# Other start places in SBUF, by 4 to 64 bytes, for the matmul operands of the SwiGLU stages of a float32r decoder trunk

## The chip, the cores and the metric

The kernel runs on one core of one Trainium2 chip. The metric is the device time of one execution in microseconds. A profiled execution is slightly shorter in its span (first to last instruction) than in the time that is reported for it.

## The reference

The reference is a decoder trunk of two layers on 256 positions of 1024 channels, all in float32. A layer is a first SwiGLU block, a mixer, and a second SwiGLU block:

```python
x = x + 0.5 * swiglu(rms_norm(x, ffn1_norm[l]), ffn1_w_gate[l], ffn1_w_up[l], ffn1_w_down[l])
...
x = x + merged @ w_out[l]
x = x + 0.5 * swiglu(rms_norm(x, ffn2_norm[l]), ffn2_w_gate[l], ffn2_w_up[l], ffn2_w_down[l])

def swiglu(x, w_gate, w_up, w_down):
    return (jax.nn.silu(x @ w_gate) * (x @ w_up)) @ w_down
```

Gate and up have 1024 x 2816 weights, down has 2816 x 1024. The mixer (a forgetting attention and a gated recurrence beside each other) is not touched by the change.

## The kernel before

**Products.** Every large product is made of three matmuls in float32r. Each operand is split into a high part, rounded to float32r, and a low part, the rest: `mm3` (L256) issues high weights with high activations, high weights with low activations, and low weights with high activations, all into one PSUM bank. A matmul has 128 x 128 weights and 256 columns of activations, which are all 256 positions; each issues its own weight load, as the profile's PEld counts show.

**Weights.** SyncE brings 1 MB pieces of weights from HBM into the three buffers `wr`. `split_half` (L378) splits one half piece, 128 x 1024, at a time: ScalarE casts it to the high part and VectorE subtracts to get the low part (`split`, L280). The parts lie in tiles of 1088 elements a partition: eight tiles `W`, or tiles of the pool of 21 called `R` when no two W tiles are idle. A part takes up 1024 of the 1088 elements, and `where` (L374) says from which element: the pair in `self.spots`, or `AT = 16, 48`, that is 64 B for the high part and 192 B for the low part. The bases of all W and R tiles are multiples of 128 B in the built program. The q, k and v projections of the mixer have (0, 0); there the weights are the moving operand, with 512 columns.

**A SwiGLU stage** (`ffn`, L607). There are four: `ffn1` and `ffn2` in both layers. The 22 blocks of 128 hidden channels each have a gate half and an up half, of 8 x 3 matmuls each, which makes 1056 matmuls for gate and up. The moving operand is `xs`, the normalised input in both parts. `glu` (L657) takes the two banks: VectorE scales the gate's, ScalarE applies SiLU, VectorE multiplies with up, and `split` writes h in two parts into an `R` tile that holds two blocks: high of the first block at element 0, low at 256, high of the second at 512, low at 768. Then the down product runs over 8 blocks of output channels, each over the 22 blocks of h: 528 matmuls, whose moving operand is h. `FFN_AT` (L59) is the pair of places for all weights of these stages, the same as `AT`.

**What sets the order.** The program is written out by a planner that runs a model of the engines' clocks (`Clock`, L66) and emits work when operands are due (`run`, L401). Its model has names and sizes of tiles, not addresses.

**The start.** `setup` (L515) issues `WARM` = 9 float32 matmuls of zeros on TensorE while the first weights are on their way. The profile records each as two.

Of the kernel before, what the change touches and what calls it, by code (L numbers as in the profile page):

```python
# [24 lines left out]
F32R = mybir.dt.float32r  # L25
# [5 lines left out]
NF = F // 128  # L31
# [2 lines left out]
OFF = {"q": 0, "k": 1024, "v": 2048, "f": 3072, "xr": 3080, "gr": 4104, "gA": 5128, "gR": 6152}  # L34
PROJ = [("q", 0), ("k", 0), ("v", 0), ("q", 1), ("k", 1), ("v", 1)]

MIX = [('q',0),('k',0),('xr',0),('v',0),('xr',1),('q',1),('k',1),('v',1),('gr',0),('gr',1),('gA',0),('gA',1),('gR',0),('gR',1)]

P_G = {"ffn1": 0, "mix": 8, "ffn2": 16}
P_QN, P_KN, P_CW, P_CB, P_BA, P_BX, P_BGA, P_BGM, P_LAM, P_BXR, P_BGR, P_BV, NP_ = 24, 25, 26, 58, 66, 74, 82, 90, 98, 106, 114, 122, 130  # L40
LEAD = 5
WARM = 9
EARLY = -0.6
ROOM = 3.5
FLEX = 4
# [7 lines left out]
EARLYX = -0.4  # L53
CALM = 2, 3
NEAR = 8
SIDES = False

AT = 16, 48
FFN_AT = AT  # L59


def f32(ap):
# [138 lines left out]
class Trunk:  # L201
# [199 lines left out]
    def run(self):  # L401
# [8 lines left out]
        for s, st in enumerate(steps):  # L410
# [6 lines left out]
            ends = any(lab == "x" for st in steps[max(0, s - CALM[1]):s + CALM[0]] for _, lab in st.done)  # L417
            while (j < n and first[j] - s <= (NEAR if ends else AHEAD) and self.split_places()
                   and self.clock.done[self.raw[j // 2].tensor.name] <= self.now + EARLY
# [95 lines left out]
    def setup(self):  # L515
# [16 lines left out]
        warm = self.take(self.banks)  # L532
        for _ in range(WARM):
            self.PE.matmul(warm[:, 0:128], self.cpad, self.cpad, start=True, stop=True)
# [72 lines left out]
    def ffn(self, l, name):  # L607
        st = {}
        phase = self.phase
        self.phase += 1  # L610

        def gu_steps(f):
            js = self.half(), self.half()
            self.spots.update(dict.fromkeys(js, FFN_AT))
            banks = {}

            def step(i, ks):
                def fn(wh, wl):
                    if ks[0] == 0:

                        self.need(lambda: phase in self.rb or len(self.banks.idle) > 1, "stats", "x")
                        banks[i] = self.take(self.banks)
                    for k in ks:
                        w = slice(k * 128, k * 128 + 128)
                        self.product(banks[i], wh[:, w], wl[:, w], self.x_rhs(phase, k), k == 0, k == 7, SIDES)
                return Step(js[i], fn, [(self.glu(f, phase, banks, st), "glu")] if i and ks[-1] == 7 else [])
            if f == 0 and not self.steps:
                order = [(i, ks) for ks in (range(4), range(4, 8)) for i in range(2)]
            elif f == 0:
                order = [(0, range(4)), (0, range(4, 7)), (1, range(4)), (1, range(4, 7)), (0, range(7, 8)), (1, range(7, 8))]  # L630
            else:
                order = [(i, ks) for i in range(2) for ks in (range(4), range(4, 8))]
            self.steps += [step(i, ks) for i, ks in order]

        for f in range(NF):
            gu_steps(f)
        halves = [self.half() for _ in range(NF)]
        self.spots.update(dict.fromkeys(halves, FFN_AT))
        runs = {}
        for i in range(8 * NF):  # L640
            d, f = divmod(i, NF)
            runs.setdefault((halves[i // 8], d, i // 4), []).append((i % 8, f))

        def down(half, d, blocks):
            def fn(wh, wl):
                for i, f in blocks:
                    if f == 0:
                        st["acc", d] = self.take(self.banks)
                    self.need(lambda: ("h", f) in st, "glu", "stats", "x")
                    w = slice(i * 128, i * 128 + 128)  # L650
                    self.product(st["acc", d], wh[:, w], wl[:, w], st["hT", f // 2][:, f % 2], f == 0, f == NF - 1, SIDES)
                    if d == 7 and f % 2:
                        self.big.give(st.pop(("tile", f // 2)))
            return Step(half, fn, [(self.ffn_end(l, name, phase, d, st), "x")] if blocks[-1][1] == NF - 1 else [])
        self.steps += [down(half, d, blocks) for (half, d, _), blocks in runs.items()]

    def glu(self, f, phase, banks, st):  # L657
        if phase not in self.rb:
            yield self.when(must=lambda: phase in self.rb)
            yield self.when(self.rb[phase])  # L660
        s2 = self.take(self.small)
        g, h = s2[:, 0:256], s2[:, 256:512]
        self.DVE.tensor_mul(g, self.total(banks[0], SIDES), self.rb[phase])
        self.banks.give(banks[0])
        self.ACT.activation(g, g, AF.Silu)
        yield self.when(s2)

        self.DVE.tensor_mul(h, self.total(banks[1], SIDES), g)
        self.banks.give(banks[1])
        if ("hT", f // 2) not in st:  # L670
            st["tile", f // 2], st["hT", f // 2] = self.slot([2, 512], F32R)
        hT = st["hT", f // 2][:, f % 2]
        yield self.when(s2)
        self.split(hT[:, 0:256], hT[:, 256:512], h)
        self.small.give(s2)
        st["h", f] = True

    def ffn_end(self, l, name, phase, d, st):
        last = name == "ffn2" and l == L - 1
        bank = st["acc", d]  # L680
        y = self.t([128, 256], "sq", 2)
        self.DVE.tensor_mul(y, self.total(bank, SIDES), self.rb[phase])
        self.banks.give(bank)
# [7 lines left out]
    def mix(self, l):  # L691
# [58 lines left out]
        on = {"xr": (self.on_xr, "rnn"), "gr": (self.on_gr, "gr"), "gA": (self.on_gate, "gate"), "gR": (self.on_gate, "gate")}  # L750
        for nm, n in MIX:
            if nm in "qkv":
# [43 lines left out]
    def block_diagonal(self, M):  # L796
        for n in range(2):
            yield self.step_at(M["base"] + 8 * MIX.index(("xr", n)) + (-8, 4)[n])
            raw, w = self.slot([4, 2, 128])
# [363 lines left out]
def _columns(w):  # L1163

    return w.reshape(8, 128, -1, 128).transpose(2, 1, 0, 3).reshape(-1, 128, 1024)


def _ffn_halves(wg, wu, wd):
    gu = np.stack([_columns(wg), _columns(wu)], axis=1).reshape(2 * NF, 128, 1024)
    dn = wd.reshape(NF, 128, 8, 128).transpose(2, 0, 1, 3).reshape(NF, 8, 128, 128)  # L1170
    return [gu, dn.transpose(0, 2, 1, 3).reshape(NF, 128, 1024)]


def _weights(a):
    out = []
    for l in range(L):
        w = a["w_in"][l]
        out += _ffn_halves(a["ffn1_w_gate"][l], a["ffn1_w_up"][l], a["ffn1_w_down"][l])
        out += [(_rows if nm in "qkv" else _columns)(w[:, OFF[nm] + 512 * n:OFF[nm] + 512 * n + 512]) for nm, n in MIX]
        out += [_columns(a[nm][l]) for nm in ("w_o_attn", "w_o_rnn", "w_out")]  # L1180
# [45 lines left out]
```

## Time and profile before

| | |
|---|---|
| time before, median of 2 runs | 1228.41 us (1227.72 to 1229.11) |
| the profiled execution: its time | 1227.54 us |
| the profiled execution: its span | 1225.8 us |
| TensorE busy | 1218.8 us, 10040 matmuls |
| TensorE loading weights | 1190.1 us |
| VectorE busy | 844.4 us |
| ScalarE busy | 698.6 us |
| GpSimd busy | 38.9 us |
| read from HBM | 229.84 MB, 188 GB/s over the span |

In the profile, PE is TensorE's matmuls and PEld its weight loads, which overlap them; DVE is VectorE, ACT is ScalarE, POOL is GpSimd. A group or row of the timeline names what an instruction writes and reads by tiles without their numbers: `B<-xs,W` is a matmul into a PSUM bank with moving operand xs and weights in a W tile. Nearly all rows carry line L158, the helper that records every operation, so they are told apart by tiles. A matmul's duration in the profile (276 ns for 256 columns) is the time through the array; since the next starts long before it ends, the time of a stretch is the distance from one start to the next. The stages follow each other on TensorE, in times from the start of the span: first SwiGLU of layer 0 from 6.8 to 190.3 us, mixer, second SwiGLU from 435.6 to 616.0, first SwiGLU of layer 1 from 616.0 to 796.5, mixer, second SwiGLU from 1041.4 to 1221.9.

### The profile page before, as it was taken

What the parts mean: (1) busy time and instruction counts of PE and PEld (TensorE: products, weight loads), DVE (VectorE), ACT (ScalarE), POOL (GpSimd) and SP (SyncE); (2) the same over time, 40 slices, a digit from 0 to 9 for tenths busy, and PEclk for the clock granted to TensorE, in tenths of its full rate; (3) what the DMA queues carried; (4) which work ended last, traced back from release to release, by engine and by line L of the source; (5) the groups of instructions that cost most, each with busy time, mean ns of one, the idle gap of its engine ahead of it and who ended that gap; (6) DMA issues with size and microseconds to landing.
All of it is one profiled execution on the core that took longest, in us unless ns stands there. A gap on an engine that the chain in (4) does not pass through costs nothing.

```text
span 1225.8 us, 24093 instructions
## 1 busy us (share of the span) xinstructions
PE 1218.8 (99%) x10040; PEld 1190.1 (97%) x10040; DVE 844.4 (69%) x1387; ACT 698.6 (57%) x1214; POOL 38.9 (3%) x48
## 2 busy tenths in 40 slices
PE   8999999999999999999999999999999999999998
PEld 8999998988999999999999999989899999999998
DVE  6765566887769776655676565668877697765553
ACT  6554445679786565444555444465887755654431
POOL 1000000101000000000000000011010000000000
PEclk9999999999999999999999999999999999999999
DMA  8665465454446566444566454654444564654451
GB/s 302 220 211 187 160 217 196 154 196 157 172 153 243 190 217 231 172 173 172 206 235 210 161 186 160 227 184 172 157 170 172 172 242 171 241 209 172 170 190 52
DMA packets 36030, 232.47 MB, mean 190 GB/s; under 512 B 4528, under 2 KB 5712, under 8 KB 9040
## 3 DMA queue, kind: packets, MB, share of 16 engines
q1 hardware_dynamic: 35776, 230.79, 53.0%
q8 instruction: 79, 1.29, 0.4%
q14 instruction: 31, 0.25, 0.1%
q10 hardware_dynamic: 144, 0.13, 0.1%
HBM read 229.84 MB, written 1.06 MB: 188 GB/s over the span
## 4 chain that ended last, share of the span: by engine, by line
PE 95%; DVE 3%; DMA 1%; issue 1%; ACT 0%; SPq 0%; DVEq 0%; ACTq 0%
PE B L158 95%; DVE R L158 2%; DVE W L158 1%; DMA R<-cd 0%; DMA wr<-ws 0%; ACT W L158 0%; DVE lg L158 0%; DVE nm L158 0%; SPq L158 0%; DVE sq L158 0%; DVE S L158 0%; DVE x L158 0%; ACT rb L158 0%; ACT S L158 0%; ACT dp L158 0%
## 5 line engine op out<-in xcount | busy, mean ns | idle before, releaser
L158 DVE TENSOR_TENSOR W<-wr,W 128x1024 fp32r<-128x1024 f32 (+1 forms) x293 | 355.0, 1214 | 176.6 <-ACT W L158 176.0
L158 PE MATMUL B<-xs,W 128*128 128x256 f32 x3768 | 449.0, 278 | 1.9 <-ACT W L158 1.5
L158 PEld LDWEIGHTS B<-xs,W 128*128 128x128 f32 x3768 | 437.5, 188 | 3.5 <-ACT W L158 1.8
L158 ACT CAST W<-wr 128x1024 fp32r<-128x1024 f32 (+1 forms) x293 | 302.0, 1039 | 167.8 <-PE B L158 133.9
L158 PE MATMUL B<-R,W 128*128 128x256 f32 x2328 | 269.7, 276 | 0.1
L158 PEld LDWEIGHTS B<-R,W 128*128 128x128 f32 x2328 | 266.5, 188 | 0.3 <-DVE R L158 0.3
L158 PE MATMUL B<-xs,R 128*128 128x256 f32 x1992 | 235.3, 276 | 0.0
L158 PEld LDWEIGHTS B<-xs,R 128*128 128x128 f32 x1992 | 230.3, 188 | 0.2
L158 DVE TENSOR_TENSOR R<-wr,R 128x1024 fp32r<-128x1024 f32 x133 | 160.9, 1219 | 37.4 <-ACT R L158 37.4
L158 ACT CAST R<-wr 128x1024 fp32r<-128x1024 f32 x133 | 136.8, 1043 | 1.7 <-DMA wr<-ws 1.7
L158 PE MATMUL B<-R,R 128*128 128x256 f32 (+1 forms) x1000 | 123.9, 279 | 0.0
L158 PEld LDWEIGHTS B<-R,R 128*128 128x128 f32 x1000 | 117.3, 188 | 0.4
L158 ACT ACTIVATE S<-S 128x256 f32<-128x256 f32 x88 | 36.3, 418 | 137.9 <-DVE S L158 137.9
L158 PE MATMUL B<-W,xs 128*128 128x512 f32 x444 | 106.5, 393 | 0.0
L158 PEld LDWEIGHTS B<-W,xs 128*128 128x128 f32 x444 | 82.4, 188 | 16.7
L158 ACT ACTIVATE xs<-x,prm 128x256 fp32r<-128x256 f32 x48 | 23.8, 508 | 82.9 <-DVE x L158 80.6
L158 DVE TENSOR_TENSOR sq<-B,rb 128x256 f32<-128x256 f32 x32 | 13.6, 425 | 70.1 <-PE B L158 70.1
L158 POOL TENSOR_TENSOR rst<-rst,mhalf 128x4 f32<-128x4 f32 (+1 forms) x22 | 30.4, 1392 | 861.9 <-DVE rst L158 861.9
L158 DVE TENSOR_TENSOR S<-B,S 128x256 f32<-128x256 f32 x88 | 36.4, 418 | 23.3 <-PE B L158 20.8
L158 DVE TENSOR_TENSOR R<-S,R 128x256 fp32r<-128x256 f32 x88 | 36.6, 421 | 21.6 <-ACT R L158 21.6
L158 ACT CAST R<-S 128x256 fp32r<-128x256 f32 x88 | 34.7, 400 | 22.0 <-DVE S L158 22.0
L158 DVE TENSOR_TENSOR S<-B,rb 128x256 f32<-128x256 f32 x88 | 36.3, 417 | 0.0
(115 smaller groups left out, 678.7 us busy)
## 6 DMA issues: line engine op xcount, KB each, us to landing
wr<-ws SPq DMA_DIRECT2D x210, 1024.0 KB, 4.8
bias<-b_in SPq DMA_DIRECT2D x8, 256.0 KB, 4.9
R<-wbd SPq DMA_DIRECT2D x4, 512.0 KB, 5.9
R<-cd SPq DMA_DIRECT2D x4, 512.0 KB, 5.5
x<-xT SPq DMA_DIRECT2D x4, 256.0 KB, 5.3
wr<-ws SPq DMA_DIRECT2D x4, 256.0 KB, 5.4
wr<-ws SPq DMA_DIRECT2D x2, 512.0 KB, 7.0
out<-x SPq DMA_DIRECT2D x8, 128.0 KB, 1.7
```

Source lines behind the costliest of these rows:

```text
L158: return fn(*args, **kw)
```

## The change

`FFN_AT` becomes a table by layer and stage. Each entry has the places of the gate and up weights (high, low), those of the down weights, and those of h (high, low, and the distance between the two blocks in a tile). All in elements of 4 B:

```diff
-FFN_AT = AT
+FFN_AT = {(0, "ffn1"): ((20, 52), AT, (4, 260, 512)), (0, "ffn2"): ((24, 56), AT, (8, 264, 512)),
+          (1, "ffn1"): ((24, 48), AT, (0, 528, 256)), (1, "ffn2"): ((16, 56), (17, 49), (0, 256, 512))}
...
-            self.spots.update(dict.fromkeys(js, FFN_AT))
+            self.spots.update(dict.fromkeys(js, FFN_AT[l, name][0]))
...
-        self.spots.update(dict.fromkeys(halves, FFN_AT))
+        self.spots.update(dict.fromkeys(halves, FFN_AT[l, name][1]))
...
-                    self.product(st["acc", d], wh[:, w], wl[:, w], st["hT", f // 2][:, f % 2], f == 0, f == NF - 1, SIDES)
+                    hh, hl = st["hT", f]
+                    self.mm3(st["acc", d][:, 0:256], wh[:, w], wl[:, w], hh, hl, f == 0, f == NF - 1)
...
-        if ("hT", f // 2) not in st:
-            st["tile", f // 2], st["hT", f // 2] = self.slot([2, 512], F32R)
-        hT = st["hT", f // 2][:, f % 2]
+        if ("tile", f // 2) not in st:
+            st["tile", f // 2] = self.take(self.big, F32R)
+        st["hT", f] = [st["tile", f // 2][:, a + at[2] * (f % 2):][:, :256] for a in at[:2]]
         yield self.when(s2)
-        self.split(hT[:, 0:256], hT[:, 256:512], h)
+        self.split(*st["hT", f], h)
...
-WARM = 9
+WARM = 6
```

Against the places before, in bytes:

| stage | gate/up weights, high and low | down weights | h, high and low |
|---|---|---|---|
| layer 0, first | +16, +16 | as before | +16, +16 |
| layer 0, second | +32, +32 | as before | +32, +32 |
| layer 1, first | +32, 0 | as before | high of both blocks ahead, then low of both, 64 B further (2112 B from the high part of its block) |
| layer 1, second | 0, +32 | +4, +4 | as before |

The list `MIX` is written out again with the same entries, and the new constant `W0` is used nowhere.

On each engine the instructions stand in the same order before and after, with the same tiles up to their running numbers, but for one row on TensorE. At the start of TensorE's queue (`cpad` is the tile of zeros, `xs` the input, `W` the weights) stood before:

```order
L158 MATMUL B_94<-cpad 128x128 x9
L158 MATMUL B_146<-xs,W_112 128x256 x2
L158 MATMUL B_146<-xs,W_113 128x256
L158 MATMUL B_146<-xs,W_112 128x256 x2
L158 MATMUL B_146<-xs,W_113 128x256
```

and now:

```order
L164 MATMUL B_94<-cpad 128x128 x6
L164 MATMUL B_143<-xs,W_109 128x256 x2
L164 MATMUL B_143<-xs,W_110 128x256
L164 MATMUL B_143<-xs,W_109 128x256 x2
L164 MATMUL B_143<-xs,W_110 128x256
```

Three matmuls of zeros are gone, which also lowers the running numbers by three; what follows is the same work from other places.

More of the change, by code (lines that the diff above doesn't have):

```diff
@@ L35 @@
 PROJ = [("q", 0), ("k", 0), ("v", 0), ("q", 1), ("k", 1), ("v", 1)]
-MIX = [('q',0),('k',0),('xr',0),('v',0),('xr',1),('q',1),('k',1),('v',1),('gr',0),('gr',1),('gA',0),('gA',1),('gR',0),('gR',1)]
+MIX = [('q', 0), ('k', 0), ('xr', 0), ('v', 0), ('xr', 1), ('q', 1), ('k', 1), ('v', 1), ('gr', 0), ('gr', 1), ('gA', 0), ('gA', 1), ('gR', 0), ('gR', 1)]
 P_G = {"ffn1": 0, "mix": 8, "ffn2": 16}
@@ L55 @@
 NEAR = 8
+MIX = [('q', 0), ('k', 0), ('xr', 0), ('v', 0), ('xr', 1), ('q', 1), ('k', 1), ('v', 1), ('gr', 0), ('gr', 1), ('gA', 0), ('gA', 1), ('gR', 0), ('gR', 1)]
+W0 = 768
 SIDES = False
 AT = 16, 48
-FFN_AT = AT
+FFN_AT = {(0, "ffn1"): ((20, 52), AT, (4, 260, 512)), (0, "ffn2"): ((24, 56), AT, (8, 264, 512)),
+          (1, "ffn1"): ((24, 48), AT, (0, 528, 256)), (1, "ffn2"): ((16, 56), (17, 49), (0, 256, 512))}
 def f32(ap):
@@ L625, in fn @@
                         self.product(banks[i], wh[:, w], wl[:, w], self.x_rhs(phase, k), k == 0, k == 7, SIDES)
-                return Step(js[i], fn, [(self.glu(f, phase, banks, st), "glu")] if i and ks[-1] == 7 else [])
+                return Step(js[i], fn, [(self.glu(f, phase, banks, st, FFN_AT[l, name][2]), "glu")] if i and ks[-1] == 7 else [])
             if f == 0 and not self.steps:
@@ L655, in ffn, with glu @@
         self.steps += [down(half, d, blocks) for (half, d, _), blocks in runs.items()]
-    def glu(self, f, phase, banks, st):
+    def glu(self, f, phase, banks, st, at):
         if phase not in self.rb:
```

## The prediction

> **What bounds the kernel now.** I read the page first: the shares of the engines, the granted clock, the chain that ended last.
>
> ```profile
> span 1225.8 us, 24093 instructions
> ...
> PE 1218.8 (99%) x10040; PEld 1190.1 (97%) x10040; DVE 844.4 (69%) x1387; ACT 698.6 (57%) x1214; POOL 38.9 (3%) x48
> ...
> PEclk9999999999999999999999999999999999999999
> ...
> PE 95%; DVE 3%; DMA 1%; issue 1%; ACT 0%; SPq 0%; DVEq 0%; ACTq 0%
> ```
>
> TensorE is busy through the span and 95% of the chain that ended last is TensorE work, so the time is the number of matmuls times the spacing of their starts. The question is which spacing. Next I cut the span into the eight half stages of the SwiGLU stages (gate and up columns, then down) and asked for the busy times in each.
>
> ```profile
> core 0: us, PE busy (x) PEld busy (x) DVE busy (x) ACT busy (x) POOL busy (x), PEclk, DMA share, GB/s
> 6.78:130.49 123.71, 123.20 (x1062) 122.26 (x1063) 87.20 (x137) 68.75 (x108) 2.26 (x3) 1.00 0.62 225
> 130.49:190.33 59.84, 59.84 (x530) 59.84 (x529) 37.65 (x52) 27.94 (x38) 0.00 (x0) 1.00 0.59 205
> 435.59:556.21 120.62, 120.62 (x1065) 120.57 (x1064) 78.93 (x117) 62.45 (x91) 1.60 (x1) 1.00 0.56 197
> 556.21:616.05 59.84, 59.84 (x531) 59.84 (x530) 37.89 (x53) 28.21 (x38) 0.00 (x0) 1.00 0.53 190
> 616.05:736.66 120.61, 120.61 (x1064) 120.56 (x1063) 77.22 (x115) 60.81 (x90) 1.61 (x1) 1.00 0.56 199
> 736.66:796.50 59.84, 59.84 (x530) 59.84 (x529) 37.54 (x52) 27.94 (x38) 0.00 (x0) 1.00 0.55 196
> 1041.41:1162.03 120.62, 120.62 (x1064) 120.57 (x1063) 78.95 (x117) 62.39 (x91) 1.61 (x1) 1.00 0.56 197
> 1162.03:1221.87 59.84, 59.84 (x530) 59.81 (x528) 26.94 (x35) 18.07 (x19) 0.00 (x0) 1.00 0.37 131
> ```
>
> The code gives each gate/up half 44 x 8 x 3 = 1056 matmuls and each down half 22 x 8 x 3 = 528 (the counts in the rows take in the neighbours at the edges and the statistics). 59.84 / 528 = 113.33 ns, four times to the last digit. The gate/up halves take 119.7 us at that spacing and show 120.6, the rest being the statistics. So 6336 of the 10040 matmuls stand in stages that wait for nobody: 718 us at one fixed spacing. Only that spacing can be changed by where the operands lie.
>
> Is 113.33 ns the least that 256 columns can take? Three looks at the timeline (start, us, engine, line, operation, operands), each a stretch and the start of what comes after it, or two windows on one stretch:
>
> ```profile
> 8.09 2.12 PE L158 MATMUL B<-xs,W 128*128 128x256 f32 x9
> ...
> 8.31 1.27 PE L158 MATMUL B<-xs,W 128*128 128x256 f32 x5
> ```
>
> ```profile
> 194.44 1.52 PE L158 MATMUL B<-R,xs 128*128 128x512 f32 x6
> 195.80 0.50 PE L158 MATMUL B<-ones,acc 128*128 128x1 f32 x4
> ...
> 201.75 2.03 PE L158 MATMUL B<-xs,wf 128*16 128x256 f32 x16
> 203.62 0.59 PE L158 MATMUL B<-sq,ones 128*128 128x256 f32 x2
> ```
>
> ```profile
> 297.01 1.65 PE L158 MATMUL B<-xs,W 128*128 128x256 f32 x12
> 298.49 0.49 PE L158 MATMUL B<-ident,lg 128*128 128x128 f32 x3
> ```
>
> In the first 10 us the array still runs slowly: (2.12 - 1.27) / 4 = 213 ns for the same 256 columns. Half of it is 106.6 ns, and the full-speed spacing is not half but 113.33. So 6.7 ns of each matmul is no array work (an estimate from these two rows). At 512 columns the spacing is 1.36 / 6 = 227 ns, twice 113.33, so the loss grows with the data streamed: 6.7 ns for 1024 B of a partition, 0.42 ns for each 64 B. That looks like the supply of operands from SBUF, and it makes their places worth a question.
>
> The third stretch is the only one where an operand does not start on a multiple of 64 B: the forget weights (wf) lie at byte 203552, which is 32 past such a multiple; every W, R, S and xs operand of the matmuls starts on one. These 16 matmuls take 1.87 / 16 = 116.9 ns each, 3.6 ns over the rest, and do so to the end of the stretch. But they also load only 16 or 8 columns of weights, so the place is not the only thing that differs. The last stretch restarts after a transpose and is spread over 1.48 / 12 = 123.3 ns each, the restart in it: for some matmuls after an interruption the spacing is off before it falls back to 113.33.
>
> **The change part by part.** *Order.* No instruction is moved, and none is added. Three warm-up matmuls (six records) are left out at the start.
>
> ```profile
> 1.11 4.21 PE L158 MATMUL B<-cpad 128*128 128x128 f32 x18 [1.11 <-DVE mhalf L158]
> 6.78 15.87 PE L158 MATMUL B<-xs,W 128*128 128x256 f32 x120 [1.45 <-ACT W L158]
> ```
>
> They end 6 x 4.21 / 18 = 1.4 us earlier, but the next matmul waits 1.45 us for ScalarE's first weights, and then waits 2.9: nothing is gained. What could be lost is speed: the first 3.3 us of real matmuls ran at 213 ns. If the array speeds up only after so much busy time, 1.4 us less of it means 1.4 us more at 213 in place of 113, which costs 1.4 x (1 - 113 / 213) = 0.7 us. Between 0 and 0.7 I take 0.3.
>
> *Writes to the new places.* ScalarE writes each high part and VectorE each low part, now 4 to 64 B further on. Neither engine's price shows a place:
>
> ```profile
> L158 DVE SCALAR_TENSOR_TENSOR R<-R,prm,R 128x256 f32<-128x256 f32 x48 | 22.7, 483 | 1.1
> L158 DVE SCALAR_TENSOR_TENSOR xs<-x,prm,xs 128x256 fp32r<-128x256 f32 x48 | 22.6, 481 | 11.5 <-ACT xs L158 11.5
> ...
> L158 ACT ACTIVATE R<-R,cb,prm 128x256 f32<-128x256 f32 x13 | 6.8, 598 | 0.0
> L158 ACT ACTIVATE R<-R,sp_neg 128x256 f32<-128x256 f32 x16 | 8.3, 594 | 0.0
> ```
>
> The first of each pair reads the convolution's rows, of 259 elements each, from places 4, 8 or 12 B off, the second reads aligned ones: 483 against 481, 598 against 594. Writes off the boundary are not shown apart; I take 0. The cover is the idle time in the windows above: VectorE works 78.9 of 120.6 us in a gate/up half, so its work there could grow by half before the matmuls wait for it. With that cover gone, each per cent on it would cost 0.8 us a half stage.
>
> *Weights.* Off a 64 B boundary now: both parts of gate and up in layer 0 (2 x 1056 matmuls), one part in layer 1 (the high one serves two of three matmuls, 704; the low one the third, 352), the down weights of the last stage (528, by 4 B). 3696 in all. Bound below: 0, or a gain if the place is what causes the 6.7 ns (a rival). Bound above: the 10.0 ns of the stretch at 297 us, and 3.6 from the stretch at 201.75. The operands that differ so far, by 64 B between weights and activations and by 128 B between high and low weights, all run at 113.33, and a shifted operand touches just one 64 B piece more, 9 for 8. I take one piece, 0.42 ns: 3696 x 0.42 = 1.6 us. The wf row is the nearer in place but not in shape, so it gets a chance of its own.
>
> *Activations of down.* Both halves of h are 16 B off in layer 0's first stage and 32 B off in its second: 1056 matmuls, 17 pieces for 16, 0.4 us, with the same bounds. In layer 1's first stage the low part moves by 64 B, a place like those that exist: 0.
>
> [...]
>
> *Sum.* 0.3 + 1.6 + 0.4 = 2.3 us. The profiled execution took 1227.54 us (span 1225.8 and 1.7 around it), which makes 1229.8; it lies 0.9 under the median of the two runs shown, 1228.41, so against the median I forecast **1230.7 us**.
>
> **The rivals.**
>
> *A: weights off the boundary cost what the wf row shows.* 3.6 ns on 3696 matmuls is 13.3 us, with the other terms (0.7) **1242.4 us**: slower, though by just over one per cent. For it: that row is the only one with such weights, and it does not settle in 16 matmuls while other stretches do. Against it: its loads are of 8 and 16 columns, which may be what it pays for. It decides as soon as one stage with both parts shifted shows 117 in place of 113.33.
>
> *B: the two streams never settle in any shifted stage.* If 113.33 is a rhythm between weight load and moving stream that holds only for places multiples of 64 B apart, all 6336 matmuls lose it. A price between 3.6 and 10.0, taken as 5 ns, makes 31.7 us: **1260 us**, slower by 2.6%. For it: the interrupted stretches show that the rhythm can be lost; the hi, hi, lo pattern of layer 1 would change the phase at each matmul. Against: down in layer 1 keeps or nearly keeps its places. It passes 2% (24.6 us) from 3.9 ns on.
>
> *C: one of the places takes the loss away.* Spacing 106.6 in one whole stage: 1584 x 6.7 = 10.6 us, **1217.8 us**. Faster by 2% needs 24.6 us / 6.7 ns = 3670 matmuls, more than two of the four stages, and as each stage tries another shift that is unlikely. For it: the loss exists and goes with the bytes. Against: at 227 ns the 512-column stretches of the projections, with weights and activations 0 B apart in place of 64, have the same loss per byte, so it has not followed the place so far. [...]
>
> *D: the 4 B shift alone is dear.* If weights that start inside an aligned group need two reads for one, the last down half could double: 528 x 113.3 = 59.8 us, **1288 us**. Nothing in the trace shows a matmul operand so placed; the reads of VectorE and ScalarE above show no such price.
>
> **How the numbers follow.** Forecast 0.54, A 0.24, C 0.10, B 0.09, D 0.03. The forecast's own range is 1226 to 1234. The range of all reaches down to about C in one stage, 1218, and up over A and the lower part of B to 1251; B's upper part, D and a wider C, some 0.16, lie outside. A measurement of this kernel can tell 2% from no change. Faster by that: the far end of C, 0.02. Slower by that: most of B, and D, 0.11. Within it: 0.87.
>
> **What would show it.** Right: the same eight half stages at 120.6 and 59.8 us, none off by more than 1 us, and the first wait on ScalarE's weights longer by 1.4 us. A is seen as gate/up halves of 124.4 us in layer 0, 123.1 and 121.9 in layer 1, and down unchanged but for the last, 61.7; B as 126 and 62.5 us everywhere; C as a half stage under 117 or under 58; D as a last half of over 100 us. I am wrong if any half stage moves by more than 2 us either way, or if VectorE or ScalarE become what the matmuls wait for.

## The result, and the profile after

| | time, us | span of the profiled execution, us |
|---|---|---|
| before, median of 2 runs | 1228.41 (1227.72 to 1229.11) | 1225.8 |
| after, median of 2 runs | 1257.51 (1256.91 to 1258.12) | 1255.2 |

The ratio is 1.0239, with a 95% interval of 1.0223 to 1.0256: slower by 2.4%, and outside the predicted range.

The page of after, in the same rows as the page of before, and below them the two groups of instructions that write the parts of the weights:

```profile
span 1255.2 us, 24081 instructions
...
PE 1247.0 (99%) x10034; PEld 1218.7 (97%) x10034; DVE 844.8 (67%) x1387; ACT 698.7 (56%) x1214; POOL 38.8 (3%) x48
...
PEclk9999999999999999999999999999999999999999
...
PE 97%; DVE 1%; DMA 1%; ACT 0%; issue 0%; SPq 0%; DVEq 0%; ACTq 0%
...
L164 DVE TENSOR_TENSOR W<-wr,W 128x1024 fp32r<-128x1024 f32 (+1 forms) x293 | 355.3, 1215 | 192.5 <-ACT W L164 191.8
...
L164 ACT CAST W<-wr 128x1024 fp32r<-128x1024 f32 (+1 forms) x293 | 302.4, 1039 | 190.6 <-PE B L164 149.6
```

The span grew by 29.4 us, TensorE's busy time by 28.2, VectorE's by 0.4 and ScalarE's by 0.1, at the same granted clock, 1.000 in both. TensorE's share of the chain that ended last rose from 95 to 97%. So no engine became a new bound: the matmuls themselves take longer. The eight half stages show where (stretch, sum, busy time of each engine, clock, DMA share, GB/s):

```profile
core 0: us, PE busy (x) PEld busy (x) DVE busy (x) ACT busy (x) POOL busy (x), PEclk, DMA share, GB/s
6.55:135.70 129.15, 128.68 (x1062) 127.99 (x1063) 87.18 (x137) 68.94 (x108) 2.26 (x3) 1.00 0.60 216
135.70:198.47 62.77, 62.77 (x530) 62.77 (x529) 37.65 (x52) 27.96 (x38) 0.00 (x0) 1.00 0.55 195
443.77:569.06 125.29, 125.29 (x1064) 125.23 (x1063) 79.20 (x117) 62.44 (x91) 1.60 (x1) 1.00 0.55 190
569.06:631.54 62.48, 62.48 (x530) 62.48 (x529) 37.76 (x52) 28.19 (x38) 0.00 (x0) 1.00 0.53 183
631.54:756.82 125.28, 125.28 (x1065) 125.23 (x1063) 77.38 (x115) 60.82 (x90) 1.61 (x1) 1.00 0.54 191
756.82:819.01 62.19, 62.19 (x531) 62.19 (x530) 37.55 (x52) 27.98 (x38) 0.00 (x0) 1.00 0.53 190
1063.85:1189.05 125.20, 125.20 (x1064) 125.15 (x1063) 79.17 (x117) 62.41 (x91) 1.60 (x1) 1.00 0.54 190
1189.05:1251.25 62.20, 62.20 (x530) 62.16 (x528) 26.85 (x34) 18.07 (x19) 0.00 (x0) 1.00 0.34 124
```

Against before the halves grew by 5.44, 2.93, 4.67, 2.64, 4.67, 2.35, 4.58 and 2.36 us, 29.6 in all. All eight lost, and nearly alike: each down half now takes 62.19 to 62.77 us for 528 matmuls, 117.8 to 118.9 ns each in place of 113.33. The gate/up halves have the same spacings in their long stretches, by the distance from start to start: 118.9 in the first, 117.8 in the other three. The mixers between them kept their length (245.3 and 244.8 us, and 245.3 and 244.9 before). Even the smallest edits cost the full price: the down half of layer 1's first stage, where only the low part of h stands 64 B elsewhere, lost 2.35 us, and the last, where only the weights moved, by 4 B, 2.36.

### The profile page after: what moved, and what is told of

Same layout as the page of the kernel before. It is cut to its first block, busy times and chain, and to the rows that moved or that the text cites. A ratio compares the mean times of both kernels' runs of the same rounds, so it can differ in the third digit from the quotient of the medians.

```text
span 1255.2 us, 24081 instructions
## 1 busy us (share of the span) xinstructions
PE 1247.0 (99%) x10034; PEld 1218.7 (97%) x10034; DVE 844.8 (67%) x1387; ACT 698.7 (56%) x1214; POOL 38.8 (3%) x48
## 4 chain that ended last, share of the span: by engine, by line
PE 97%; DVE 1%; DMA 1%; ACT 0%; issue 0%; SPq 0%; DVEq 0%; ACTq 0%
PE B L164 97%; DVE R L164 1%; DVE W L164 0%; DMA R<-cd 0%; DMA prm<-prm 0%; ACT W L164 0%; DVE lg L164 0%; DVE nm L164 0%; ACT xs L164 0%; DVE sq L164 0%; DVE x L164 0%; ACT rb L164 0%; ACT S L164 0%; ACT dp L164 0%; DVE S L164 0%
## 5 line engine op out<-in xcount | busy, mean ns | idle before, releaser
L164 DVE TENSOR_TENSOR W<-wr,W 128x1024 fp32r<-128x1024 f32 (+1 forms) x293 | 355.3, 1215 | 192.5 <-ACT W L164 191.8
L164 PE MATMUL B<-xs,W 128*128 128x256 f32 x3768 | 459.8, 281 | 3.0 <-ACT W L164 2.5
L164 PEld LDWEIGHTS B<-xs,W 128*128 128x128 f32 x3768 | 448.0, 189 | 4.5 <-ACT W L164 2.8
L164 ACT CAST W<-wr 128x1024 fp32r<-128x1024 f32 (+1 forms) x293 | 302.4, 1039 | 190.6 <-PE B L164 149.6
L164 PE MATMUL B<-R,W 128*128 128x256 f32 x2328 | 277.1, 279 | 0.0
L164 PEld LDWEIGHTS B<-R,W 128*128 128x128 f32 x2328 | 273.9, 188 | 0.2 <-DVE R L164 0.2
L164 PE MATMUL B<-xs,R 128*128 128x256 f32 x1992 | 244.3, 281 | 0.0
L164 PEld LDWEIGHTS B<-xs,R 128*128 128x128 f32 x1992 | 238.9, 189 | 0.2
L164 PE MATMUL B<-R,R 128*128 128x256 f32 (+1 forms) x1000 | 126.7, 282 | 0.0
L164 PEld LDWEIGHTS B<-R,R 128*128 128x128 f32 x1000 | 120.1, 189 | 0.4
```

The lines of the kernel that those rows point to most:

```text
L164: return fn(*args, **kw)
```

## The experiments

All kernels are the changed kernel with another table of places, which is written here in short (`AT` stands for (16, 48)). Its program differs from that of before in the places alone once `WARM` is 9 again, as it is unless a diff below says otherwise. An entry reads (gate/up weights high, low), (down weights high, low), (h high, low, distance of blocks), in elements of 4 B. Where the input is moved too, by `XS_AT` elements in the phases layer 0 first, mixer, second, layer 1 first, mixer, second, this is the edit:

```diff
-        self.xs = self.t([128, 8, 512], "xs", 1, F32R, self.ops)
+        self.xs = self.view(self.t([128, 4160], "xs", 1, F32R, self.ops), [8, 512], XS_AT[phase])
```

"Distance" is the place of a matmul's weights less the place of its activations, in bytes modulo 128. Before, it is 64 for all three matmuls of a product (weights at 64 and at 192, activations at multiples of 256). Since every half stage stands for itself, one run tries eight placements, and a half stage tells its spacing: 59.84 us of a down half or 120.6 of a gate/up half is 113.33 ns, 62.2 or 125.3 is 117.8 ns.

The first four runs set three theories against each other. **R**: the distance counts, and 64 is the good one. **P**: the absolute places count, and operands must stand where they stood. **M**: it is enough that the three matmuls of a product have one distance.

### e1: other distances, and shifts of both operands of down

```diff
+FFN_AT = {(0, "ffn1"): ((0, 32), (20, 52), (4, 260, 512)),
+          (0, "ffn2"): ((18, 50), (32, 64), (16, 272, 512)),
+          (1, "ffn1"): ((48, 16), (24, 56), (8, 264, 512)),
+          (1, "ffn2"): ((32, 64), (16, 48), (16, 272, 512))}
```

> Each half stage tries another pair of places; the time of a half stage tells (gate/up 120.6 us where the spacing is 113.3 ns, 125.2 at 118; down 59.8 or 62.3). Theory R (only the distance of weights from activations counts, and 64 B modulo 128 is the good one): gate/up of layer 0 first (weights at 0 and 128 B, distance 0) 125; gate/up of layer 0 second (distance 72) 125; gate/up of layer 1 first (high and low places exchanged, distance still 64) 120.6; gate/up of layer 1 second (weights at 128 and 256 B, distance 0) 125; the downs of layer 0 first (weights and h both 16 B on), layer 0 second (both 64 B on) and layer 1 first (both 32 B on) 59.8, the last (h alone 64 B on, distance 0) 62.3. Theory P (absolute places count: activations at a multiple of 128 B, weights 64 B past one): the gate/up halves as under R, but all four downs 62.3. Theory M (any distance will do if it is the same in all three matmuls of a product): every half stage 120.6 or 59.8.

Measured: 1254.57 us, against 1227.94 for before on the same chip. The windows (stretch, sum, TensorE busy, clock, DMA share, GB/s), from layer 0's first down half on:

```profile
136.38:198.56 62.18, 62.18 (x530) 1.00 0.54 196
443.75:569.17 125.42, 125.42 (x1064) 1.00 0.54 191
569.17:629.03 59.86, 59.86 (x530) 1.00 0.53 186
629.03:755.23 126.20, 126.20 (x1065) 1.00 0.53 191
755.23:815.10 59.87, 59.87 (x530) 1.00 0.56 197
1060.13:1185.97 125.84, 125.84 (x1065) 1.00 0.54 190
1185.97:1248.86 62.89, 62.89 (x530) 1.00 0.34 122
```

Weights and h moved together by 64 B (third row) or by 32 B (fifth) keep 59.86: P falls, and a start off a 64 B boundary is free there. But moved together by 16 B (first row) they lose, which R does not allow. Distance 0 loses in both gate/up halves that have it, though it is the same in all three matmuls (sixth row; the other, layer 0's first, took 129.50 us), and h moved alone by 64 B loses too (last row), though all its operands stand on multiples of 64 B. M falls. The fourth row, with high and low weights exchanged, is odd: its first 42 matmuls ran at 113.33, those after each of two later restarts at 118.9.

### e2: the parts of the change one by one

```diff
+WARM = 6
+FFN_AT = {(0, "ffn1"): (AT, AT, (0, 260, 512)), (0, "ffn2"): ((16, 16), AT, (4, 288, 544)),
+          (1, "ffn1"): ((28, 60), AT, (0, 512, 256)), (1, "ffn2"): ((17, 49), (17, 48), (0, 256, 512))}
```

> Parts of the change alone, with 6 warm-up matmuls. Gate/up of layer 0 first has the old places and shows the warm-up alone: 120.6 plus the start as before, within 1 us, under all theories. Gate/up of layer 0 second: both parts at 64 B, distance 64: 120.6 under R, P and M. Gate/up of layer 1 first: 48 B on (distance 112): 125 under R and P, 120.6 under M. Gate/up of layer 1 second: 4 B on: 125 under R and P, 120.6 under M. Down of layer 0 first: only the low part of h 16 B on (one matmul of three): R, P and M 61 to 62.3. Down of layer 0 second: only the high part of h 16 B on (two of three): 61 to 62.3 under all. Down of layer 1 first: the new layout of h (both high parts, then both low) without its 64 B: 59.8 under all; 62.3 would say that the layout and not the place costs. Down of layer 1 second: only the high weights 4 B on: 61 to 62.3 under all.

In layer 0's first stage four elements of every second h are overwritten by the next block's; the amount of work is the same.

Measured: 1246.0 us. Three of its windows: both weights at 64 B; the layout of h of layer 1's first stage without the extra 64 B; the high down weights alone moved by 4 B.

```profile
438.54:559.34 120.80, 120.80 (x1065) 1.00 0.55 196
...
747.36:807.20 59.84, 59.84 (x530) 1.00 0.57 195
...
1177.57:1240.34 62.77, 62.77 (x530) 1.00 0.35 123
```

So 128 B between high and low weights is not needed for 113.33 ns, though with both at 64 B a stretch of 51 matmuls ran at 117.8. The layout of h costs nothing by itself, and moving one operand alone is as dear as moving more: the two gate/up halves of layer 1, with the weights alone moved by 48 and by 4 B, took 125.25 and 125.28 us, against M. The low part of h alone by 16 B, which serves one of the three kinds of matmul, made 62.18, its high part alone 62.77. The gate/up half at the old places but after six warm-up matmuls took 124.67 us against 123.71 in before's trace, and its granted clock was 0.99, against 1.00. That is not put down to the three missing warm-ups: the first gate/up halves of e1, e3, e4 and e7, with nine, were at 0.99 as well, and those of after and e9, with six, at 1.00.

### e3: everything moved together, and two parts alone

```diff
+FFN_AT = {(0, "ffn1"): ((20, 52), (20, 52), (4, 260, 512)),
+          (0, "ffn2"): ((24, 56), (24, 56), (8, 264, 512)),
+          (1, "ffn1"): ((32, 64), (32, 64), (16, 272, 512)),
+          (1, "ffn2"): ((16, 48), (16, 52), (0, 256, 512))}
+XS_AT = [4, 0, 8, 16, 0, 16]
```

> Weights and activations are shifted together, the input tile too: by 16 B in layer 0's first stage, 32 B in its second, 64 B in layer 1's first; in the last stage the input alone is 64 B on (gate/up at distance 0) and the down's low weights alone 16 B on. R: the first three stages as before the change (gate/up 120.6, the first 123.7, down 59.8), the last 125 and 61 to 62.3, and 1234 us in all. P: all eight half stages as after the change, 125 and 62.3, and 1257 us in all. M: 1228 us plus at most 2.5 for the last down.

Measured: 1242.86 us (4 runs), ratio 1.0123 (1.0106 to 1.014).

```profile
134.73:196.92 62.19, 62.19 (x531) 1.00 0.56 196
442.21:562.87 120.66, 120.66 (x1064) 1.00 0.56 196
562.87:622.71 59.84, 59.84 (x530) 1.00 0.54 190
622.71:743.37 120.66, 120.66 (x1065) 1.00 0.55 199
743.37:803.21 59.84, 59.84 (x531) 1.00 0.57 196
1048.02:1174.67 126.65, 126.65 (x1065) 1.00 0.54 189
1174.67:1236.85 62.18, 62.18 (x530) 1.00 0.36 123
```

All operands moved by 16 B lose (first row, and the gate/up half ahead of it with 128.11 us), by 32 B keep (next two), by 64 B keep (next two). The input moved alone by 64 B loses 6.0 us (sixth), and the low down weights alone by 16 B lose 2.3 (last). Neither R nor P gives this time: it takes the right distance, and a shared shift of 32 or 64 B in place of 16.

### e4: the forget weights on a multiple of 64 B

The rows of the forget weights (wf) were the place where the prediction weighed shape against place. Here the second tile of wf, the one the timeline names with 16 columns, stands with every slice 64 B past a multiple of 128, and in layer 1 the weights of q, k and v, which are the moving operand there, stand at (64, 192) in place of (0, 0). The table tries weights moved alone by other amounts.

```diff
-            self.spots.update(dict.fromkeys(js, (0, 0)))
+            self.spots.update(dict.fromkeys(js, [(0, 0), (16, 48)][l]))
...
-        M["wf2"] = self.t([128, 8, 16], "wf2", 1, F32R)
+        M["wf2"] = self.view(self.t([128, 264], "wf2", 1, F32R), [8, 32], 8)[:, :, 0:16]
...
+FFN_AT = {(0, "ffn1"): ((4, 36), (18, 50), (0, 256, 512)), (0, "ffn2"): ((16, 52), (20, 52), (0, 256, 512)),
+          (1, "ffn1"): ((12, 44), (24, 56), (0, 256, 512)), (1, "ffn2"): ((20, 48), (32, 64), (0, 256, 512))}
```

> The forget weights lie 64 B past a multiple of 128 B for every slice, in place of 32 and 96: if their place made the 116.9 ns of those 16 matmuls, R and P expect 113.3 now; if their few columns make it (M, or a third cause), 116.9 stays. In layer 1 the weights of q, k and v, which are the moving operand there, start at 64 and 192 B in place of 0: R and P leave open what it does, M expects no change in the settled spacing of 226.7 ns. Half stages: gate/up at distances 16, 64 with 80 for the low part, 48, and 80 for the high part with 64 for the low: all 125 under R and P; 120.6 for the first and third under M. Downs with weights 8, 16, 32 and 64 B on: all 62.3 under R and P, 59.8 under M.

Measured: 1261.71 us. The timeline of before in layer 1's mixer, and then that of e4, in the same place (start, us, engine, line, operation, operands, count):

```profile
803.82 4.26 PE L158 MATMUL B<-W,xs 128*128 128x512 f32 x18
807.92 2.03 PE L158 MATMUL B<-xs,wf 128*16 128x256 f32 x16
809.79 0.59 PE L158 MATMUL B<-sq,ones 128*128 128x256 f32 x2
```

```profile
829.96 4.31 PE L166 MATMUL B<-W,xs 128*128 128x512 f32 x18
834.11 1.99 PE L166 MATMUL B<-xs,wf 128*16 128x256 f32 x16
835.94 0.59 PE L166 MATMUL B<-sq,ones 128*128 128x256 f32 x2
```

From start to start, the same 16 matmuls on 16 and 8 columns of weights take 1.87 / 16 = 116.9 ns before and 1.83 / 16 = 114.4 now (113.8 in layer 0; after the first two each is at 113.33). The shape is the same, so it was the place that the wf row had paid for. The 512-column matmuls went the other way: 4.10 / 18 = 227.8 ns before, 4.15 / 18 = 230.6 now. In layer 0, where they kept distance 0, they settle at 226.7 ns; in layer 1 no stretch settles, most of them at 229 to 230. So the distance that is good at 256 columns is not good at 512.

All eight half stages lose: gate/up took 125.25 to 128.62 us, down 62.19 to 63.36. The two down halves with weights moved by 8 and by 16 B took 63.35 us, 120.0 ns a matmul.

### e5 and e6: which pairs count, and which shared shifts

Two pairs of theories were left. **O**: each matmul's own weights must stand at distance 64 from its own activations; **N**: it is the weights loaded next, during the stream of the one before, whose distance counts. **E**: shared shifts must be multiples of 32 B; **F**: with the distance right, every shift will do.

```diff
+FFN_AT = {(0, "ffn1"): ((48, 48), (16, 32), (0, 528, 256)), (0, "ffn2"): ((16, 32), (16, 0), (0, 528, 256)),
+          (1, "ffn1"): ((16, 48), (16, 48), (0, 544, 256)), (1, "ffn2"): ((48, 16), (16, 16), (0, 544, 256))}
+XS_AT = [0, 0, 0, 32, 0, 32]
```

> Theory N: what counts is the distance, modulo 256 B, from a streaming operand to the weights that are loaded while it streams, those of the next matmul: high weights against high activations (good at 64 B) and low weights against low activations (good at 64 or 192 B). Theory O: what counts is the distance of each matmul's own weights from its own activations; the pair high weights, low activations then has to be 64 as well. Down of layer 0 first: low h 64 B on, low weights at 128 B, so N sees 64 and 64, O sees 0 and 128: N 59.8, O 62.2 or more. Down of layer 0 second: low h 64 B on, low weights at 0, N sees 64 and 192: N 59.8, O 62.2 or more. Down of layer 1 first: low h 128 B on, N sees 64 and 64: N 59.8, O sees 192 for high weights and low h and expects 62.2. Down of layer 1 second: low h 128 B on, low weights as the high ones at 64, N sees 64 and 192: N 59.8, O 62.2. Gate/up: both weights at 192: N 125; weights at 64 and 128 (N sees 64 and 128): 125; the input 128 B on with the old weights (192 and 64, as with the places exchanged): 125; the input 128 B on and the places exchanged (64 and 192 again): 120.6 under N and O if only distances count. In the q, k and v projections the weights stream with 512 columns: in layer 0 at 192 and 64 B (N sees 64 and 192) N expects 226.7 ns settled, in layer 1 both at 64 B (192 and 192) N expects 229 to 230 as in the run before.

Measured: 1250.16 us (before 1228.64 on that chip). All four down halves lost, so N's expectations for them were missed:

```profile
569.08:631.27 62.19, 62.19 (x530) 1.00 0.53 183
631.27:752.44 121.17, 121.17 (x1064) 1.00 0.57 197
752.44:816.26 63.82, 63.82 (x530) 1.00 0.53 186
1061.62:1182.27 120.65, 120.65 (x1065) 1.00 0.56 196
```

The two kept halves are gate/up halves whose input moved by 128 B, the second with high and low weights exchanged, which makes it the old pattern 128 B on; it kept 113.33 throughout. In the first of them, expected at 125 us, the early stretches ran at 119 ns and the long one, after a restart, at 113.33. The third row, with the low part of h another 128 B further, lost the most, although each distance is 64; the last down half, with the same h and both weights at 64 B, took 62.18 us. The gate/up half with both weights at 192 B, layer 0's first, lost as well: it ended at 134.93 us of the span, and at 130.49 in before; both at 64 B, in e2, took 120.80. The moving weights of q, k and v, at (192, 64) in layer 0 and at (64, 64) in layer 1, lost in both: 231 and 229 ns, where N had expected 226.7 for the first.

```diff
+FFN_AT = {(0, "ffn1"): ((28, 60), (28, 60), (12, 268, 512)), (0, "ffn2"): ((24, 24), (17, 49), (1, 257, 512)),
+          (1, "ffn1"): ((64, 32), (40, 8), (24, 280, 512)), (1, "ffn2"): ((0, 0), (18, 50), (2, 258, 512))}
+XS_AT = [12, 0, 8, 48, 0, 48]
```

> All distances are kept good (64 and 192, or 64 and 64, as N counts them); only where both operands lie together is changed. Theory E: a pair shifted together keeps its rhythm if the shift is a multiple of 32 B, and loses it otherwise. Theory F: 16 B was lost for another reason and only the distance counts. Gate/up of layer 0 first, 48 B on together: E 127 to 128, F 123.7; its down, 48 B on together: E 62.2, F 59.8. Gate/up of layer 0 second, 32 B on together with both weight parts at one distance: 120.6 under both; its down, 4 B on together: E 62.2, F 59.8. Gate/up of layer 1 first, 192 B on together: 120.6 under both; its down, 96 B on together: 59.8 under both. Gate/up of layer 1 second, 192 B on together with both weight parts at one distance: 120.6 under both; its down, 8 B on together: E 62.2, F 59.8. Projections of 512 columns: layer 0 with streaming weights at 128 and 128 B, layer 1 at 0 and 128 B; neither theory has a number, the settled spacing is looked up: 226.7 is good, 229 to 230 is lost.

Measured: 1249.25 us.

```profile
443.82:568.75 124.93, 124.93 (x1064) 1.00 0.54 191
568.75:632.89 64.14, 64.14 (x531) 1.00 0.53 178
...
753.54:813.44 59.90, 59.90 (x530) 1.00 0.55 196
...
1180.21:1243.58 63.37, 63.37 (x530) 1.00 0.35 124
```

Shared shifts of 4 B (second row, 121.5 ns, the dearest of all), 8 B (last, 120.0) and 48 B (62.19) lose, 96 B (third) and 192 B (the gate/up half ahead of it, 120.65) keep: among the shifts tried E holds, and F falls. The exception is the first row, moved by 32 B with both weights at one place: its first two stretches ran at 113.3, the long one after a restart at 117.8. That made a further question of whether one placement can have two states. The projections of 512 columns lost too: with the moving weights at (128, 128) in layer 0 and at (0, 128) in layer 1 the stretches ran at 231 to 233 ns. So distance 0 modulo 128 isn't enough for them; only the old places, (0, 0), kept 226.7 in any run.

### e7: all operands of all four stages moved together

```diff
+P64 = ((32, 64), (32, 64), (16, 272, 512))
+P32 = ((24, 56), (24, 56), (8, 264, 512))
+FFN_AT = {(0, "ffn1"): P64, (0, "ffn2"): P64, (1, "ffn1"): P32, (1, "ffn2"): P32}
+XS_AT = [16, 0, 16, 8, 0, 8]
```

> Every operand of the four SwiGLU stages is moved, the input tile and h too: by 64 B in layer 0 and by 32 B in layer 1, so that all distances stay 64 B modulo 128. If the distance and a multiple of 32 B are all that count, every half stage is as before the change (123.7, then 120.6 and 59.8) and the time is 1228 us within 2; if absolute places count, 1257 us as with the change.

Measured: 1228.41 us (10 runs) against 1228.10 (13 runs), ratio 1.000 (0.999 to 1.0009).

```profile
131.11:190.95 59.84, 59.84 (x530) 1.00 0.58 204
436.53:557.15 120.62, 120.62 (x1064) 1.00 0.57 196
...
737.62:797.47 59.85, 59.85 (x531) 1.00 0.56 196
1042.71:1163.37 120.66, 120.66 (x1064) 1.00 0.56 196
```

Every operand of 6336 matmuls stands elsewhere than before, half of them off a 64 B boundary, and the time is the same. What the change lost, it lost by moving the operands against each other: in each of its eight half stages one of them stayed where it was.

### e8: broken stretches

**B** here says that a placement can have two states, chosen anew at each restart; **S**, that the places alone decide. A matmul into another bank, whose result isn't used, breaks each gate/up half into stretches:

```diff
+                        if i == 0 and f in (5, 8, 11, 14, 17):
+                            pt = self.take(self.banks)
+                            self.PE.matmul(pt[:, 0:128], self.ident, self.ident, start=True, stop=True)
+                            self.banks.give(pt)
...
+FFN_AT = {(0, "ffn1"): (AT, AT, (0, 256, 512)), (0, "ffn2"): ((24, 24), AT, (0, 256, 512)),
+          (1, "ffn1"): ((48, 16), AT, (0, 256, 512)), (1, "ffn2"): ((24, 56), AT, (0, 256, 512))}
+XS_AT = [0, 0, 8, 0, 0, 0]
```

> In each gate/up half five small float32 matmuls of a constant tile (128 columns, result unused) break the stream, ahead of blocks 5, 8, 11, 14 and 17. Theory B (two states): with places where a 113.3 ns rhythm exists, a break is a new throw, and the stretch after it can be at 113.3 or at 117.8 to 118.9 until the next break; with places where none exists, no break helps. Layer 0 first, old places: every stretch settles within 12 matmuls. Layer 0 second (both weight parts 64 B from the input, all 32 B on; its longest stretch was at 117.8): some of its stretches at 113.3, some lost. Layer 1 first (high and low places exchanged; it was at 118.9): some of each. Layer 1 second (weights 32 B on alone, distance 96): none settles. Rival S (the state is a matter of places alone): layer 0 second and layer 1 first are lost in every stretch, or settled in every one.

Measured: 1240.9 us. The windows go from break to break, 144 matmuls each; four in layer 0's second stage (both weights at distance 64), one in layer 1's second (distance 96):

```profile
465.94:482.50 16.56, 16.56 (x148) 1.00 0.67 230
482.50:499.68 17.18, 17.18 (x148) 1.00 0.53 182
499.68:516.25 16.57, 16.57 (x149) 1.00 0.47 162
516.25:533.43 17.18, 17.18 (x148) 1.00 0.51 168
1078.13:1095.31 17.18, 17.18 (x148) 1.00 0.66 233
```

One placement, two durations: 16.56 us is 144 x 113.33 ns and 0.24 for the break, 17.18 is 144 x 117.8 and 0.22. A break can change the state, and the state lasts to the next break. Whether chance decides it is not shown: the kernel was run once, and in layer 0's second stage the two states took turns. With high and low exchanged, settled, lost, lost and then five times settled. At the old places every stretch settles at 113.33 ns once the slow first matmuls are past (213 ns in the first 10 us of before); at distance 96, none of eight. The down halves behind them, at the old places, took 59.84 to 59.88 us: a lost state isn't carried into the next half stage. B holds and S falls, for the two placements tried here with distance 64 other than the old pattern; that the choice is random, as B says, stays open.

### e9: the changed weights alone

```diff
+FFN_AT = {(0, "ffn1"): ((20, 52), AT, (0, 256, 512)), (0, "ffn2"): ((24, 56), AT, (0, 256, 512)),
+          (1, "ffn1"): ((24, 48), AT, (0, 256, 512)), (1, "ffn2"): ((16, 56), (17, 49), (0, 256, 512))}
```

> The change with h put back to its old places: weights alone are shifted, 6 warm-up matmuls as with the change. If the half stages are independent, the downs of layer 0 and of layer 1's first stage fall back to 59.8 us, and the time is the change's less 2.9, 2.6 and 2.4: 1249.6 us. If a lost rhythm of gate/up is carried into the down that follows, these downs stay at 62 and the time at 1257.

Measured, with the change's `WARM` of 6: 1248.62 us (2 runs), ratio 1.0164 (1.0143 to 1.0184). The three down halves with h back at its old places are at 59.86 to 59.88 us, the last one stays at 62.19, and the gate/up halves at 128.39, 125.29, 125.27 and 125.21. The halves add up independently: 1257.51 less 2.9, 2.6 and 2.3 is 1249.7, which is 1.1 over the measured time; 0.8 of that is the first gate/up half, with 128.39 us in place of 129.15.

### e10: the lost placements, broken

The breaks of e8, and one ahead of each of the blocks 1 to 7 of down:

```diff
+                    if f == 0 and d:
+                        pt = self.take(self.banks)
+                        self.PE.matmul(pt[:, 0:128], self.ident, self.ident, start=True, stop=True)
+                        self.banks.give(pt)
...
+FFN_AT = {(0, "ffn1"): ((20, 52), (16, 32), (0, 528, 256)), (0, "ffn2"): ((28, 60), (16, 0), (0, 528, 256)),
+          (1, "ffn1"): (AT, AT, (0, 544, 256)), (1, "ffn2"): (AT, (20, 52), (4, 260, 512))}
+XS_AT = [4, 0, 12, 0, 0, 0]
```

> Breaks as in the run before (five in each gate/up half, and now one ahead of each of the seven later output blocks of down) give each place eight throws or so; a place for which a 113.3 ns rhythm exists should show it in some stretch. Down of layer 0 first (low h 64 B on, low weights at 128 B) and second (low h 64 B on, low weights at 0): N (the weights loaded while an operand streams must be 64 B or 192 B from it) expects settled stretches, O (each matmul's own weights must be 64 B modulo 128 from its own activations; here high weights against low h are 0) expects none. Down of layer 1 first (low h 128 B on): both expect some. Theory E (both operands at multiples of 32 B): gate/up of layer 0 first (all 16 B on), second (all 48 B on) and down of layer 1 second (all 16 B on): no settled stretch; F (distance alone): some. Gate/up of layer 1, both, old places: every stretch settled.

Measured: 1258.8 us (before 1227.82 on that chip). One block of 66 matmuls in two of the down halves, and one stretch of 144 in layer 0's and in layer 1's second gate/up half:

```profile
765.31:773.50 8.19, 8.19 (x71) 1.00 0.46 144
...
1197.08:1205.08 8.00, 8.00 (x71) 1.00 0.41 148
...
474.25:491.44 17.19, 17.19 (x149) 1.00 0.68 229
1095.44:1112.04 16.60, 16.60 (x149) 1.00 0.70 246
```

A settled block would take 66 x 113.33 = 7.48 us and the break. None of the stretches with shared shifts of 16 or 48 B settles anywhere (gate/up of layer 0: 0 of about 11, and 0 of 8; the last down: 0 of 8), so E is not a matter of the state that a stretch fell into. The down halves of layer 0, where only N has its good distances, don't settle either (0 of 8 each; 8.04 and 8.00 us a block), so N falls. Of O one half stands: every placement of a half stage that settled anywhere has each matmul's own weights 64 B modulo 128 from its own activations. The other half doesn't, since that isn't enough: the low part of h 128 B further (first row), with all three distances at 64, was expected to settle in some blocks and did in none. The gate/up halves of layer 1, at the old places, settle in all eight stretches.

### The placements side by side

For matmuls of 256 columns, over all runs:

| own weights less own activations, modulo 128 B | common shift | spacing, ns |
|---|---|---|
| 64, pattern of before | 0, 32, 64, 96, 128, 192 B | 113.33, always |
| 64, both weights in one place, or high and low exchanged, or the input alone 128 B on | multiples of 32 B | 113.33 or 117.8 to 119, by stretch (both at 192 B: lost in its one half stage) |
| 64, low h another 128 B further | 0 | 120 to 121 (both weights at 64 B: 117.8), always |
| 64, pattern of before | 4, 8, 16, 48 B | 121.5, 120.0, 117.8, 117.8, always |
| another in one of the three matmuls or in all | any tried | 117 to 120, always |

## Why the prediction was wrong

**What bounds the kernel** was read rightly. TensorE's spacing in the SwiGLU stages sets the time, and the 29.4 us are 6336 matmuls x 4.64 ns.

**The step that failed is the price of the weights' and activations' places.** The prediction bounded it between 0 and 10.0 ns a matmul and chose "one piece, 0.42 ns", with the ground that operands that "differ so far, by 64 B between weights and activations and by 128 B between high and low weights, all run at 113.33". That sentence counts several places, but all the 256-column rows behind it had one and the same distance, 64 modulo 128: they were one sample, not several, and said nothing about other distances. e1 and e3 show the price, 4.4 ns and more, at the distances that differ. The three terms taken at 0.42 ns or at 0 measured 4.4 to 5.6:

- weights, 3696 x 0.42 = 1.6 us in the sum: e9, with these alone, lost 20.5 us against before, in the same four gate/up halves and the last down;
- activations of down, 0.4 us: 2.9 and 2.6 in the two halves of layer 0;
- layer 1's first down, "a place like those that exist: 0": 2.35 us. The place existed, but not the pair; e2 shows the same layout without the 64 B at no cost.

The number of matmuls was wrong too. The prediction charged those whose operand was moved, 3696 and 1056. The trace of after shows that a whole half stage loses its rhythm when one of its three kinds of matmul is off, and e2 shows it with the low part of h alone, e3 with the low down weights alone.

**Rival B happened**, with a chance of 0.09. Its place and its time were right: all eight half stages, forecast at 126 and 62.5 us, came at 125.2 to 125.3 (129.15 in the first) and 62.2 to 62.8; 5 ns gave 1260, 4.64 gave 1257.5. Its condition was wrong: not "places multiples of 64 B apart", since distance 0 and shifts by 64 B alone lose too. The argument against it, that "down in layer 1 keeps or nearly keeps its places", fell with the 2.35 us of those two halves.

**Rival A was refused on the wrong ground.** "Its loads are of 8 and 16 columns, which may be what it pays for": e4 shows that the wf rows pay for their place, 116.9 ns there and 113.8 to 114.4 with the same columns 64 B past a multiple of 128. Had that row been read as a matter of place, its 3.6 ns on all 6336 matmuls would have given 22.8 us, not the 13.3 of A, which counted only weights off a 64 B boundary.

**Rival C** fell: no placement in 88 half stages of after and the experiments went under 59.84 us for down. The 6.7 ns was the author's estimate, from half of the 213 ns of the first matmuls; no run shows a spacing of 106.6. Its ground against, that the 512-column stretches lose the same per byte at distance 0, compared two shapes: 256 columns at distance 0 run at 118.3 and 119.1 ns (the long stretches of the two gate/up halves of e1). **Rival D** fell: the last down half took 62.20 us, not 100. A shift of 4 B does not double anything; shared by both operands it was the dearest, at 8.1 ns a matmul.

**The writes** at 0 were right: VectorE's low parts took 1215 ns (1214 before) and ScalarE's high parts 1039 (1039). **The warm-up** at 0.3 us can't be told from nothing: the first real matmul starts 0.23 us earlier, the wait on ScalarE's first weights grew by 1.0 us, from 1.5 to 2.5, where 1.4 was foreseen, and the first gate/up half varied from 123.7 to 124.7 us among the kernels at settling places (before, e2, e7). **The order** moved nothing, as said.

**What stays open** is what in the chip makes the rhythm. The runs show a spacing that holds for as long as nothing interrupts, two states of one placement, and a dependence on the distance and on 32 B. The distance modulo 128 does not tell all: moving the input alone by 128 B, or the low part of h, changed what was kept (to 119 ns in some stretches, and to 63.82 us for a down half). The runs don't show whether one of the two streams of operands waits for the other, what decides the state after a break, why 512 columns kept their spacing at the places (0, 0) alone, or why the low part of h 128 B further never settles. No kernel here was faster than the kernel before; e7 equals it.

## What to carry to other kernels

Where TensorE's spacing sets the time, the relative place of a float32r matmul's weights and activations in SBUF can matter; here it was worth 4 to 7% of a 256-column matmul (117.8 to 120.9 ns in place of 113.33). Choose it on purpose, keep it through any change of tile layout, and check it by start-to-start distances stage by stage, several placements to a kernel. Rows that share one setting are one sample, however many they are; before taking them as evidence that a thing doesn't matter, look for one row that differs in it. The single odd row in the trace should be tested by moving its operand, not argued away.

## What the runs showed of the hardware that was not expected

- Between identical instructions on one engine, without a wait, there were two lasting spacings, 113.33 and 117.8 ns, for one and the same placement; a single other matmul between them switched from one to the other (e8: 16.56, 17.18, 16.57 and 17.18 us for 144 matmuls each).
- Which places are good depends on the number of columns streamed: distance 64 B modulo 128 at 256 columns (113.33 ns), and at 512 only the old places, (0, 0), of those tried (226.7 ns; 229 to 233 at (64, 192), (192, 64), (64, 64), (128, 128) and (0, 128)).
- The shared shifts tried that are not a multiple of 32 B (4, 8, 16 and 48 B) lose 4.4 to 8.1 ns a matmul, in every stretch of every run that had them.
